# Values of all heads in one product with the tokens stationary, and an output step split behind the reciprocal

## The chip, the cores and the metric

The kernel runs on one core of a Trainium2 chip. The metric is the device time of one execution in microseconds; of several timed executions the median is given. The core's engines work side by side, each through its own queue in order: TensorE (PE, matrix products; PEld is its weight load), VectorE (DVE), ScalarE (ACT), GpSimd (POOL) and SyncE (SP, which issues the loads). A product writes to a bank of PSUM, from which VectorE or ScalarE must take the result before the bank is used again.

## The reference

The reference computes one layer of a hybrid streaming encoder for two request groups that share their weights: a prompt of 1024 tokens and a sample of 64 tokens with running state. Per layer there are three token mixers (HGRN2, a convolution, a pool mixer) from one combined input projection, then cross attention over 256 memory tokens, then an MLP with squared ReLU, each with a residual and RMS norms. What matters here is the HGRN2 mixer:

```python
z = h @ w_in
q, fl, iv, og, ca, cg, pu = jnp.split(z, IN_SPLITS, axis=-1)
...
f_gate = lbh + (1.0 - lbh) * jax.nn.sigmoid(fh)
log_f = jnp.log(jnp.maximum(f_gate, F_FLOOR))
kh = (1.0 - lbh) * jax.nn.sigmoid(-fh)
S_new, o = hgrn2_recurrence(hg_state.astype(f32), qh, kh, vh, log_f)
o = rms_norm(o, hg_norm_g.reshape(HG_HEADS, HG_DK)).reshape(B, T, HG_WIDTH)
a_out = (o * jax.nn.silu(og.astype(f32))).astype(h.dtype)
```

There are 4 heads of 128. The values `iv` are the projection's columns 1024 to 1535. The recurrence is `S_t = diag(f_t) S_{t-1} + k_t v_t^T`, `o_t = S_t^T q_t`, and each head's output is normed over its 128 channels.

## The kernel before, in words

All 1088 tokens (1024 + 64) go through one pass. Activations lie channel-major: a tile has 128 channels as partitions and the tokens as columns. Every large product is made from three products of rounded parts, high x high, high x low and low x high, so each weight tile and each activation is split into `hi` and `lo` by a ScalarE copy and a VectorE subtraction (`prep`, `hl`).

`dense` (line 210 records every product through `mm`) multiplies one block of 128 output channels: the weights are the stationary operand, the tokens stream in three groups of 364, 364 and 360 columns, and each group takes 8 blocks of input channels x 3 = 24 products into one bank `psd`. Weight tiles come by `fetch` (a load of 512 KB on SyncE's queue, four buffers `wr`) and `prep` (three buffers `wh` and `wl`); `weights` keeps up to three ready.

In `mixers` the blocks follow each other as gates of the convolution (4 dense blocks), then per head f, q and v, with the two pool inputs behind head 1, and the four output gates og. Beside these dense blocks run background chains, Python generators: `conv` (62 steps on VectorE, lines 645 and 141, tile `cacc`, then its norm), one `head` per head, and `pool` (GpSimd additions, line 137, tiles `ws` and `wu`). After each of the three column groups of a dense block `pump` advances each chain by a third of its rate: 2 for convolution and pool, 5 for a head. A newly inserted head goes to the front of the list.

A head's chain consists of these pieces, each ending in a `yield`: the diagonal scores (line 516); nine transposes of the values `vT` to token-major `vt` (lines 528, 531) with their evacuations; seven levels (line 545, with small products of lines 556 and 562), in each of which VectorE copies the scores by a mask (line 511) and multiplies `fn` and `q` by the decays `tot` before the next level can start; transposes of the keys (line 585); the chunk states `st` (line 597); and three output parts. An output part makes `o` in a bank (lines 623, 625), squares it with a sum on ScalarE, takes the root (ScalarE, which loads another table when root and sigmoid alternate), the reciprocal `hr` on VectorE (line 629), scales `o` on ScalarE, transposes it on TensorE (line 634) and evacuates it as `on`.

In the mixers no order is written out by hand. The framework's scheduler orders the instructions of each engine by its own costs and the place in the program, and the engines then run these queues strictly in order.

Of the kernel before, what the change touches and what calls it, by code (L numbers as in the profile page):

```python
# [52 lines left out]
class Trunk:  # L53
# [378 lines left out]
    def mixers(self, xs):  # L432
# [33 lines left out]
        for h in range(NH):  # L466
            sig = self.slot(n="fs")
            sgn = self.slot(n="fn")

            def evf(b, t0, m):  # L470
                self.act(sig[:, t0:t0 + m], b, AF.Sigmoid)
                self.act(sgn[:, t0:t0 + m], b, AF.Sigmoid, scale=-1.0)
            self.dense(self.weights(), xs, ks, evf)
            f = sig[:, :T]
            nc.vector.tensor_scalar(f, f, self.lb1[:, h:h + 1], self.lb[:, h:h + 1], MUL, ADD)
            nc.vector.tensor_scalar(f, f, FLOOR, None, MAX)
            nc.vector.tensor_scalar(sgn[:, :T], sgn[:, :T], self.lb1[:, h:h + 1], None, MUL)
            q = self.slot(n="q")

            def evq(b, t0, m):  # L480
                self.act(q[:, t0:t0 + m], b, AF.Sigmoid)
                self.tt(q[:, t0:t0 + m], b, q[:, t0:t0 + m], MUL)
            self.dense(self.weights(), xs, ks, evq)
            vT = self.slot(n="vT")
            self.dense(self.weights(), xs, ks, plain(vT, AF.Copy))
            self.bg.insert(0, self.chain(self.head(h, sig, sgn, q, vT, ons), 5))
            if h == 1:
                self.pool_in(xs, ks, mix)
        for h in range(NH):
# [10 lines left out]
            self.tt(mix[h][:, :T], mix[h][:, :T], ons[h][:, :T], MUL)  # L500
        return mix

    def head(self, h, f, k, q, vT, ons):
        nc = self.nc
        mm = nc.tensor.matmul
        sc = self.slot(n="sc")
# [12 lines left out]
        mm(ps[:TS, :TS], k[:, TP:T], q[:, TP:T], start=True, stop=True)  # L519
        copy_in(sc[:TS, TP:T], self.masks[:TS, 7, :TS], ps[:TS, :TS])  # L520
        yield

        vt = self.slot(n="vt")
        for j in range(2):
            ps = self.bank("m")
            for c in range(4):
                t0 = (4 * j + c) * P
                nc.tensor.transpose(ps[:, c * P:c * P + P], vT[:, t0:t0 + P], self.ident)
            self.act(vt[:, 512 * j:512 * j + 512], ps, AF.Copy)
        ps = self.bank("m")  # L530
        nc.tensor.transpose(ps[:TS, :P], vT[:, TP:T], self.ident)
        self.act(vt[:TS, TP:TP + P], ps[:TS, :P], AF.Copy)
        self.tt(q[:, :T], q[:, :T], f[:, :T], MUL)
        tot_t = self.slot(n="tot")
        tot = f[:, :T]
# [77 lines left out]
        for t0, n in SEGS:  # L613
            w = min(n, P)
            nt = n // w
            o = self.slot(n="o")
            ps = self.bank("m")
            r = self.tp.tile([P, 8], F32, tag="hr", name=self.name("hr"))
            for c in range(nt):
                s = t0 + c * P  # L620
                first = s == 0
                prev = self.state[:, h, :] if s == TP else st[:, s - P:s]
                mm(ps[:w, c * P:c * P + P], sc[:w, s:s + w], vt[:w, s:s + P], start=True, stop=first)  # L623
                if not first:
                    mm(ps[:w, c * P:c * P + P], q[:, s:s + w], prev, start=False, stop=True)  # L625
            for c in range(nt):
                self.act(o[:w, c * P:c * P + P], ps[:w, c * P:c * P + P], AF.Square, accum_out=r[:w, c:c + 1])
            self.act(r[:w, 4:4 + nt], r[:w, :nt], AF.Sqrt, scale=1.0 / P, bias=self.eps[:w])
            nc.vector.reciprocal(r[:w, 4:4 + nt], r[:w, 4:4 + nt])
            for c in range(nt):  # L630
                self.act(o[:w, c * P:c * P + P], ps[:w, c * P:c * P + P], AF.Copy, scale=r[:w, 4 + c:5 + c])
            ps = self.bank("m")
            for c in range(nt):
                nc.tensor.transpose(ps[:, c * P:c * P + w], o[:w, c * P:c * P + P], self.ident[:w, :w])  # L634
            self.act(on[:, t0:t0 + n], ps[:, :n], AF.Copy, scale=self.vec("hg_g", h))
            yield
# [575 lines left out]
    def all_weights(self):  # L1212
        a = self.a
        for o in range(8):
            yield "c", a["wk"][o]
        for k in range(8):
            yield "c", a["wv"][k]
        for o in range(22):
            yield "c", a["w_in"][o]
        for o in range(8):  # L1220
            yield "c", a["w_out"][o]
        for o in range(8):
            yield "c", a["xq"][o]
        for _ in range(2):
            for o in range(8):
                yield "c", a["xo"][o]
        for p in list(range(NPAIR)) + list(range(LATE)):
            for j in range(2):
                yield "s", a["w_up"][2 * p + j]
        for fb in FBS:  # L1230
            for o in range(4):
                yield "c", a["w_down"][fb, o]
# [36 lines left out]
def layout(i):  # L1269
    import numpy as np  # L1270

    def c(x):
        return np.ascontiguousarray(x)
# [12 lines left out]
    ca, cg, pu = [16, 17], [18, 19], [20, 21]  # L1286
    order = [cg[0], ca[0], cg[1], ca[1]]
    for h in range(NH):
        order += [f[h], q[h], v[h]]
        if h == 1:  # L1290
            order += pu
    order += og
    a["w_in"] = c(np.stack([w_in[o] for o in order]))
    a["wk"] = blocks(i["xk_w"][0])
    a["wv"] = c(i["xv_w"][0].reshape(KT, P, KT, P))
    w_out = blocks(i["w_out"][0])
# [74 lines left out]
```

## Time and profile before

| | |
|---|---|
| three timed runs, median (range) | 1576.73 us (1575.55 to 1577.51) |
| the profiled execution, its own time | 1575.83 us |
| its span in the profile | 1574.0 us |
| mean granted clock of TensorE in it | 0.991 |
| convolution steps on VectorE (line 141, `cacc`) | 60 of 1446 ns |
| VectorE busy from 160 to 200 us, 200 to 240 us | 33.9 us, 28.5 us |

A page of the profile gives busy time per engine, a chain of waits that ended last, and groups of instructions with their mean time and the idle time ahead of them. The time lines give for each instruction its start, length, engine, line, tiles written and read, and in brackets the idle time ahead of it and what ended it. Products on TensorE overlap: each lasts about twice as long as the distance between two starts. In the tables of stretches each engine has its busy time and instructions, and behind them stand the granted clock (1.00 is full speed), the share of the DMA engines and GB/s.

### The profile page before, as it was taken

To read this page: it belongs to the slowest core of one execution; us is meant where nothing else is said; L and a number is where in the kernel's file an instruction comes from. 1 tells how busy PE (TensorE), PEld (TensorE's weight loads), DVE (VectorE), ACT (ScalarE), POOL (GpSimd) and SP (SyncE) were. 2 spreads that over 40 slices of the span, in tenths; PEclk is the share of its full clock that TensorE was granted. 3 is DMA by queue.
4 is the path that set the end of the run, shared out by engine and by line. 5 is a ranking of instruction groups with operands and counts; after the bars stand their busy time and mean duration, and the time that the engine had idled before them with its cause. 6 is when DMAs were issued, how large, how long until landed. Compare 5 with 4: busy or idle time off the path is not lost.

```text
span 1574.0 us, 24480 instructions
## 1 busy us (share of the span) xinstructions
PE 1536.2 (98%) x10312; PEld 1498.8 (95%) x10312; DVE 912.9 (58%) x1305; ACT 582.8 (37%) x1054; POOL 164.1 (10%) x125
## 2 busy tenths in 40 slices
PE   7999999899999999999998999999999999999997
PEld 7799999799999999989997999999999999999997
DVE  7628879765654433584579655555585444434434
ACT  7522242445262221373455344444362121111133
POOL 0100002200000000000023422222220000000005
PEclk9999999999999999999999999999999999999998
DMA  9421000000014311222532233222386223211003
GB/s 343 144 76 42 28 31 30 29 28 31 28 52 155 132 55 54 68 68 101 181 135 96 97 111 105 104 97 87 107 303 249 104 97 111 86 65 52 31 0 115
DMA packets 54943, 150.61 MB, mean 96 GB/s; under 512 B 6704, under 2 KB 14384, under 8 KB 54832
## 3 DMA queue, kind: packets, MB, share of 16 engines
q1 hardware_dynamic: 51952, 148.37, 27.0%
q8 instruction: 81, 1.33, 0.3%
q10 hardware_dynamic: 2880, 0.66, 0.2%
q14 instruction: 30, 0.25, 0.0%
HBM read 115.11 MB, written 33.91 MB: 95 GB/s over the span
## 4 chain that ended last, share of the span: by engine, by line
PE 64%; issue 26%; DVE 6%; ACT 2%; POOL 1%; DMA 1%; SPq 0%; POOLq 0%; ACTq 0%; DVEq 0%
PE psd L210 45%; PE psm L210 12%; PE psm L545 3%; DVE cacc L141 1%; DVE wl L138 1%; POOL xr L137 1%; DVE t L141 1%; ACT hi L126 1%; DVE x L138 1%; PE psd L865 1%; PE psm L516 0%; PE psm L623 0%; DMA wr<-wk 0%; PE psm L634 0%; PE psm L625 0%
## 5 line engine op out<-in xcount | busy, mean ns | idle before, releaser
L210 PE MATMUL psd<-hi,wh 128*128 128x364 f32 (+2 forms) x1632 | 537.9, 331 | 1.5 <-ACT hi L126 0.8
L210 PE MATMUL psd<-lo,wh 128*128 128x364 f32 (+2 forms) x1632 | 538.3, 330 | 0.9 <-DVE lo L141 0.9
L210 PE MATMUL psd<-hi,wl 128*128 128x364 f32 (+2 forms) x1632 | 538.4, 330 | 0.3 <-DVE wl L138 0.3
L126 ACT ACTIVATE wh<-wr 128x1024 fp32r<-128x1024 f32 (+1 forms) x179 | 161.4, 906 | 492.8 <-PE psd L210 350.0
L210 PEld LDWEIGHTS psd<-hi,wh 128*128 128x128 f32 x1632 | 307.2, 188 | 3.6 <-ACT hi L126 1.5
L210 PEld LDWEIGHTS psd<-lo,wh 128*128 128x128 f32 x1632 | 307.8, 189 | 2.1 <-DVE lo L141 1.5
L210 PEld LDWEIGHTS psd<-hi,wl 128*128 128x128 f32 x1632 | 307.3, 188 | 1.4 <-DVE wl L138 0.6
L138 DVE TENSOR_TENSOR wl<-wr,wh 128x1024 fp32r<-128x1024 f32 (+1 forms) x179 | 189.4, 1062 | 125.5 <-ACT wh L126 125.2
L138 DVE TENSOR_TENSOR xr<-psd,xr 128x364 f32<-128x364 f32 (+3 forms) x192 | 101.9, 533 | 177.3 <-PE psd L210 177.2
L210 PE MATMUL psd<-th,wh 128*128 128x272 f32 x448 | 130.9, 292 | 3.6 <-ACT t L126 3.3
L210 PE MATMUL psd<-th,wl 128*128 128x272 f32 x448 | 130.4, 292 | 2.8 <-DVE wl L138 2.8
L210 PE MATMUL psm<-th,wh 128*128 128x272 f32 x448 | 130.4, 291 | 1.3 <-ACT t L126 0.6
L210 PE MATMUL psm<-th,wl 128*128 128x272 f32 x448 | 129.3, 290 | 0.7 <-DVE wl L138 0.7
L210 PE MATMUL psd<-tl,wh 128*128 128x272 f32 x448 | 129.5, 289 | 0.0
L210 PE MATMUL psm<-tl,wh 128*128 128x272 f32 x448 | 128.8, 288 | 0.0
L210 PEld LDWEIGHTS psd<-th,wh 128*128 128x128 f32 x448 | 84.9, 189 | 4.8 <-ACT t L126 4.3
L210 PEld LDWEIGHTS psd<-th,wl 128*128 128x128 f32 x448 | 84.8, 190 | 3.5 <-DVE wl L138 3.5
L141 DVE SCALAR_TENSOR_TENSOR cacc<-glu,vecs,cacc 128x1118 f32<-128x1118 f32 x60 | 86.8, 1446 | 0.7
L210 PEld LDWEIGHTS psm<-th,wh 128*128 128x128 f32 x448 | 84.3, 188 | 2.7 <-ACT t L126 1.4
L210 PEld LDWEIGHTS psm<-th,wl 128*128 128x128 f32 x448 | 84.1, 188 | 1.0 <-DVE wl L138 0.9
L210 PEld LDWEIGHTS psd<-tl,wh 128*128 128x128 f32 x448 | 84.9, 190 | 0.0
L210 PEld LDWEIGHTS psm<-tl,wh 128*128 128x128 f32 x448 | 84.4, 188 | 0.0
(238 smaller groups left out, 2297.6 us busy)
## 6 DMA issues: line engine op xcount, KB each, us to landing
wr<-w_up SPq DMA_DIRECT2D x38, 512.0 KB, 3.6
tt<-t SPq DMA_DIRECT2D x32, 544.0 KB, 3.1
t<-tt SPq DMA_DIRECT2D x32, 544.0 KB, 5.0
wr<-w_down SPq DMA_DIRECT2D x32, 512.0 KB, 3.3
wr<-w_in SPq DMA_DIRECT2D x22, 512.0 KB, 3.2
x<-res SPq DMA_DIRECT2D x16, 544.0 KB, 2.9
wr<-xo SPq DMA_DIRECT2D x16, 512.0 KB, 3.4
x<-xT SPq DMA_DIRECT2D x8, 544.0 KB, 8.2
```

Source lines behind the costliest of these rows:

```text
L126: return self.inorder("act", lambda: self.nc.scalar.activation(out, in_, f, **kw))
L137: return self.inorder("pool", lambda: eng.tensor_tensor(out, a, b, op))
L138: return self.inorder("dve", lambda: self.nc.vector.tensor_tensor(out, a, b, op))
L141: return self.inorder("dve", lambda: self.nc.vector.scalar_tensor_tensor(out, in0, s, in1, op0, op1))
L210: return self.inorder("pe", lambda: self.nc.tensor.matmul(*args, **kw))
L545: mm(pv[:m, c], k[:, c * P:c * P + m], qc[:, :, 1, :], start=True, stop=True)
L865: self.nc.tensor.transpose(ps[:, i * w:i * w + w], pr[:w, i, mt * P:mt * P + P], self.ident[:w, :w])
```

## The change

There are two edits, with what they entail.

The values of all heads come from one new function, `values`, that is called once, behind head 0's q. It takes four weight tiles `w_v` at once (three from the ready ones, a fourth split into two slots `wv`), and makes the product with the tokens stationary: for each of nine tiles of 128 tokens (the last of 64) and each of 8 channel blocks three products with 512 weight columns, two token tiles and two banks at a time. The result is token-major, so `vt` of each head is a copy of 128 columns from the bank; the v blocks and the transposes of `vT` go. The list of weight loads and the weight layout follow.

The head's chain gets a `yield` between the reciprocal and the scaling of `o`, so that each of the three output parts is two pieces, and its rate is 7 instead of 5.

```diff
             self.dense(self.weights(), xs, ks, evq)
-            vT = self.slot(n="vT")
-            self.dense(self.weights(), xs, ks, plain(vT, AF.Copy))
-            self.bg.insert(0, self.chain(self.head(h, sig, sgn, q, vT, ons), 5))
+            if h == 0:
+                vts = self.values(xs)
+            self.bg.insert(0, self.chain(self.head(h, sig, sgn, q, vts[h], ons), 7))
...
+    def values(self, xs):
+
+        while len(self.wq) < 3:
+            self.prep()
+        ws, self.wq = self.wq, []
+        raw = self.raws.pop(0)[1]
+        hi, lo = (self.slot(F32R, n="wv")[:, :1024].rearrange("p (k n) -> p k n", k=KT) for _ in range(2))
+        self.act(hi, raw, AF.Copy)
+        self.split_lo(lo, raw, hi)
+        self.fetch()
+        ws = [[x.rearrange("p k n -> p (k n)") for x in w] for w in ws + [(hi, lo)]]
+        vts = [self.slot(n="vt") for _ in range(NH)]
+        for c0, c1 in ((0, 2), (2, 4), (4, 6), (6, 8), (8, 9)):
+            banks = [self.bank("d") for _ in range(c0, c1)]
+            for k in range(KT):
+                wh, wl = (x[:, 512 * (k % 2):512 * (k % 2) + 512] for x in ws[k // 2])
+                for b, (t0, m) in zip(banks, TT[c0:c1]):
+                    self.mm3_t(b[:m], xs[k][0][:, t0:t0 + m], xs[k][1][:, t0:t0 + m], wh, wl, k == 0, k == KT - 1)
+            for b, (t0, m) in zip(banks, TT[c0:c1]):
+                for h in range(NH):
+                    self.act(vts[h][:m, t0:t0 + P], b[:m, h * P:h * P + P], AF.Copy)
+            self.pump(1 if c0 % 4 else 2)
+        for _ in range(2):
+            self.prep()
+        return vts
+
-    def head(self, h, f, k, q, vT, ons):
+    def head(self, h, f, k, q, vt, ons):
...
         yield
-
-        vt = self.slot(n="vt")
-        for j in range(2):
-            ps = self.bank("m")
-            for c in range(4):
-                t0 = (4 * j + c) * P
-                nc.tensor.transpose(ps[:, c * P:c * P + P], vT[:, t0:t0 + P], self.ident)
-            self.act(vt[:, 512 * j:512 * j + 512], ps, AF.Copy)
-        ps = self.bank("m")
-        nc.tensor.transpose(ps[:TS, :P], vT[:, TP:T], self.ident)
-        self.act(vt[:TS, TP:TP + P], ps[:TS, :P], AF.Copy)
         self.tt(q[:, :T], q[:, :T], f[:, :T], MUL)
...
             nc.vector.reciprocal(r[:w, 4:4 + nt], r[:w, 4:4 + nt])
+            yield
             for c in range(nt):
                 self.act(o[:w, c * P:c * P + P], ps[:w, c * P:c * P + P], AF.Copy, scale=r[:w, 4 + c:5 + c])
...
-        for o in range(22):
+        for o in range(18):
             yield "c", a["w_in"][o]
+            if o == 5:
+                for u in range(4):
+                    yield "c", a["w_v"][u]
```

The scheduler makes new queues out of this for all engines in the mixers. Three places follow. Line numbers in the changed kernel are 15 or 16 higher in the head's function (line 629 is 644, 634 is 650, 545 is 560).

VectorE, head 1, second output part. Before, from the last of the pool steps `ws` to the reciprocal of that part (the second `hr`; `fs` and `fn` are head 2's gates):

```order
L141 SCALAR_TENSOR_TENSOR ws_2167<-wu_2168,vecs,pu_1875 128x64
L141 SCALAR_TENSOR_TENSOR cacc_1829<-glu_964,vecs,cacc_1829 128x1118
L475 TENSOR_SCALAR fs_2233<-fs_2233,lbs 128x1088
L141 SCALAR_TENSOR_TENSOR cacc_1829<-glu_964,vecs,cacc_1829 128x1118
L476 TENSOR_SCALAR fs_2233<-fs_2233 128x1088
L141 SCALAR_TENSOR_TENSOR cacc_1829<-glu_964,vecs,cacc_1829 128x1118
L629 RECIPROCAL hr_2348<-hr_2348 128x4
L477 TENSOR_SCALAR fn_2234<-fn_2234,lbs 128x1088
```

The same place in the changed kernel:

```order
L138 TENSOR_TENSOR pe_2484<-wu_2317,vecs 128x16
L141 SCALAR_TENSOR_TENSOR ws_2316<-wu_2317,vecs,pu_1965 128x1008
L138 TENSOR_TENSOR ws_2316<-pe_2484,pu_1965 128x16
L141 SCALAR_TENSOR_TENSOR ws_2316<-wu_2317,vecs,pu_1965 128x64
L644 RECIPROCAL hr_2375<-hr_2375 128x4
L644 RECIPROCAL hr_2444<-hr_2444 64x1
L475 TENSOR_SCALAR fs_2397<-fs_2397,lbs 128x1088
L682 TENSOR_REDUCE lr_2526<-psm_2521 128x2
L476 TENSOR_SCALAR fs_2397<-fs_2397 128x1088
```

The convolution steps have left this place, and the reciprocals of the second and the third part now stand ahead of the steps on head 2's gates.

ScalarE, the same output part (`o`, `hr` of head 1; `fs`, `fn` the evacuations of head 2's gates). Before:

```order
L126 ACTIVATE o_2346,hr_2348<-psm_2347 128x128 x4
L126 ACTIVATE fn_2234<-psd_2384 128x360
L126 ACT_TABLE_LOAD
L126 ACTIVATE hr_2348<-hr_2348,eps 128x4
L126 ACTIVATE wh_2440<-wr_1882 128x1024
L126 ACTIVATE o_2346<-psm_2347,hr_2348 128x128 x4
```

In the changed kernel:

```order
L126 ACTIVATE o_2373,hr_2375<-psm_2374 128x128 x4
L126 ACT_TABLE_LOAD
L126 ACTIVATE fs_2397<-psd_2405 128x364
L126 ACT_TABLE_LOAD
L126 ACTIVATE hr_2375<-hr_2375,eps 128x4
L126 ACT_TABLE_LOAD
L126 ACTIVATE fn_2398<-psd_2405 128x364
L126 ACTIVATE o_2373<-psm_2374,hr_2375 128x128 x4
```

Two evacuations and three table loads now stand between the squares and the scaled copies, where one of each and a weight copy stood. On TensorE, 40 dense products lie between the last product of this part and its first transpose, and 33 lay there before.

VectorE at the end of the value product in the changed kernel (`cacc` are the convolution's two accumulators, `wl` the low parts of the next three weight tiles, `sc` and `q` head 0's):

```order
L141 SCALAR_TENSOR_TENSOR cacc_1116<-glu_788,vecs,cacc_1116 128x1118
L141 SCALAR_TENSOR_TENSOR cacc_1543<-glu_964,vecs,cacc_1543 128x1118
L138 TENSOR_TENSOR wl_1549<-wr_1159,wh_1548 128x1024
L141 SCALAR_TENSOR_TENSOR cacc_1543<-glu_964,vecs,cacc_1543 128x1118
L138 TENSOR_TENSOR wl_1555<-wr_1252,wh_1554 128x1024
L138 TENSOR_TENSOR wl_1563<-wr_1258,wh_1562 128x1024
L141 SCALAR_TENSOR_TENSOR cacc_1543<-glu_964,vecs,cacc_1543 128x1118 x2
L138 TENSOR_TENSOR tot_1613<-fs_1054 128x544
L141 SCALAR_TENSOR_TENSOR cacc_1543<-glu_964,vecs,cacc_1543 128x1118
L537 COPY_PREDICATED sc_1595<-masks,psm_1597 128x512
```

Ahead of these rows, back to the split of the third value tile (`wl_1249`), stand 31 convolution steps and the first step of the second accumulator; before, 7 such steps stood between two splits in the v block.

More of the change, by code (lines that the diff above doesn't have):

```diff
@@ L1288, in layout @@
     for h in range(NH):
-        order += [f[h], q[h], v[h]]
+        order += [f[h], q[h]]
         if h == 1:
@@ L1293, in layout @@
     a["w_in"] = c(np.stack([w_in[o] for o in order]))
+    a["w_v"] = c(i["w_in"][0][:, 1024:1536].reshape(4, 2, P, 512).transpose(0, 2, 1, 3).reshape(4, P, KT, P))
     a["wk"] = blocks(i["xk_w"][0])
```

## The prediction

> **What bounds the kernel now.** I read the page first, then the waits of TensorE in the mixer stage, then the time lines of the engines around the one large wait there. The page's first rows:
>
> ```profile
> span 1574.0 us, 24480 instructions
> PE 1536.2 (98%) x10312; PEld 1498.8 (95%) x10312; DVE 912.9 (58%) x1305; ACT 582.8 (37%) x1054; POOL 164.1 (10%) x125
> ```
>
> TensorE is busy for nearly the whole span, so a change pays only where it takes work off TensorE or ends one of its few waits. In the stretch from 80 to 470 us, which holds the edited stage, the waits of TensorE are these:
>
> ```profile
> PE psm L634 <- ACT o L126: 6.2, 2, 6.1
> ...
> PE psm L545 <- DVE q L138: 0.4, 2, 0.3
> ```
>
> One wait is the whole matter: a transpose of line 634 stands at the head of TensorE's queue until ScalarE has scaled `o`. Who was late is seen on the time lines (start, length, engine, line, tiles, idle time before):
>
> ```profile
> 279.95 0.28 ACT L126 ACTIVATE o<-psm 128x128 f32<-128x128 f32 x1
> 280.95 0.51 ACT L126 ACTIVATE fn<-psd 128x360 f32<-128x360 f32 x1
> 281.47 1.28 ACT L126 ACT_TABLE_LOAD   x1
> 282.77 0.30 ACT L126 ACTIVATE hr<-hr,eps 128x4 f32<-128x4 f32 x1
> 290.63 1.14 ACT L126 ACTIVATE o<-psm,hr 128x128 f32<-128x128 f32 x4 [6.62 <-DVE hr L629]
> ...
> 281.57 2.56 DVE L475 TENSOR_SCALAR fs<-fs,lbs 128x1088 f32<-128x1088 f32 x1
> 284.05 2.22 DVE L141 SCALAR_TENSOR_TENSOR cacc<-glu,vecs,cacc 128x1118 f32<-128x1118 f32 x1
> 286.19 3.03 DVE L476 TENSOR_SCALAR fs<-fs 128x1088 f32<-128x1088 f32 x1
> 289.14 1.37 DVE L141 SCALAR_TENSOR_TENSOR cacc<-glu,vecs,cacc 128x1118 f32<-128x1118 f32 x1
> 290.44 0.17 DVE L629 RECIPROCAL hr<-hr 128x4 f32<-128x4 f32 x1
> ...
> 280.55 3.00 POOL L137 TENSOR_TENSOR ws<-wu 128x1111 f32<-128x1111 f32 x1
> 285.15 3.49 POOL L137 TENSOR_TENSOR wu<-ws 64x1103 f32<-64x1103 f32 x1
> ...
> 291.06 0.48 PE L634 MATMUL psm<-ident,o 128*128 128x128 f32 x1 [6.07 <-ACT o L126]
> ```
>
> The root of the norm was there at 283.1, but the reciprocal of 0.17 us came at 290.4, since four long VectorE steps stood ahead of it, and three of these ran while GpSimd computed (2.56, 2.22 and 3.03 us; the fourth took 1.37). TensorE idled 6.07 us, and then its clock was down:
>
> ```profile
> 291.00:296.00 5.00, 4.95 (x16) 3.74 (x17) 3.97 (x5) 3.29 (x9) 0.00 (x0) 0.50 0.31 108
> ```
>
> The column after POOL's is the granted clock, 0.50: five microseconds at half speed lose 2.5. This one wait thus costs 6.1 + 2.5 = 8.6 us. Nothing else in the stage is worth as much, and TensorE is otherwise back to back there.
>
> **The change, term by term.** The sum is made against the profiled execution, 1575.83 us, of which 1574.0 are the span; the median of the three timed runs, 1576.73, lies 0.90 above it, and I add that at the end.
>
> *The value product, +1.2 us.* Removed are 4 heads x 3 column groups x 24 = 288 products of 364 or 360 columns; added are 9 token tiles x 8 blocks x 3 = 216 products of 512 columns. The chain of waits has both speeds (start, length, what):
>
> ```profile
> 36.55 5.47 PE psm L210 x24
> 85.89 73.38 PE psd L210 x440
> ```
>
> The first is the memory-value product, whose form (128 stationary tokens, 512 weight columns) is the new one: 0.228 us each, so 216 take 49.2. The second gives 0.1668, so 288 take 48.0. The last token tile has 64 tokens and still runs 24 full products (5.5 of the 49.2); no row shows 64 stationary columns at 512, and I take the same speed, because the columns streamed are the same. Bounds: +1 to +2.
>
> *The transposes of the values, -3.9 us.* Per head nine go (lines 528, 531):
>
> ```profile
> 165.34 1.03 PE L528 MATMUL psm<-ident,vT 128*128 128x128 f32 x8
> 166.21 0.27 PE L531 MATMUL psm<-ident,vT 128*64 128x128 f32 x1
> 166.31 1.90 PE L545 MATMUL psm<-q,fn 128*128 128x64 f32 x16
> ```
>
> From 165.34 to 166.31 are 0.97 us, four times 3.9. Their evacuations go too. The 36 new small copies out of the value product cost ScalarE about 36 x 0.28 = 10 us (row below), hidden, since ScalarE has 49 us for them and each pair of banks is read while the next pair fills.
>
> ```profile
> L126 ACT ACTIVATE o<-psm 128x128 f32<-128x128 f32 (+1 forms) x36 | 9.5, 279 | 7.8 <-PE psm L625 7.8
> L126 ACT ACT_TABLE_LOAD x18 | 23.1, 1283 | 0.3
> ```
>
> *The large wait, -8.6 us.* In the new order the reciprocal of head 1's second part stands ahead of line 475's step, with no convolution step near it: that work has moved forward into the value product, where VectorE has little else. And between the last product that feeds the squares and the first transpose stand 40 dense products (33 before): 40 x 0.1668 = 6.7 us of cover. The chain they must cover runs on ScalarE, whose order now has three table loads in it: squares 1.0 (279.95 to 280.95), 3 x 1.28, a root 0.30, two evacuations of 0.5, the first scaled copy 0.3: 6.4 us. So the wait goes, with 0.3 us to spare. If the cover failed, I would lose up to these 8.6 again (first rival).
>
> *New short waits, +3.5 us.* The chain rate of 7 instead of 5 puts a head's levels nearer to each other: mostly 14 to 17 dense products between two of them, where 20 to 24 stood. What must fit there is VectorE's predicated copy and two multiplications (the columns are the same; a copy row of x2 has a small one at its end):
>
> ```profile
> 231.43 1.38 DVE L511 COPY_PREDICATED sc<-masks,psm 128x512 f32<-128x512 uint8 x2 [1.43 <-PE psm L545]
> 232.62 0.75 DVE L138 TENSOR_TENSOR fn<-fn,fs 128x544 f32<-128x544 f32 x1
> 233.29 0.71 DVE L138 TENSOR_TENSOR q<-q,fs 128x544 f32<-128x544 f32 x1
> ...
> 238.04 1.39 DVE L138 TENSOR_TENSOR fn<-fn,tot 128x544 f32<-128x544 f32 x1
> 239.35 1.64 DVE L138 TENSOR_TENSOR q<-q,tot 128x544 f32<-128x544 f32 x1
> ...
> 244.27 0.77 DVE L511 COPY_PREDICATED sc<-masks,psm 128x512 f32<-128x512 uint8 x2
> 244.97 0.71 DVE L138 TENSOR_TENSOR fn<-fn,tot 128x544 f32<-128x544 f32 x1
> 245.60 0.71 DVE L138 TENSOR_TENSOR q<-q,tot 128x544 f32<-128x544 f32 x1
> ...
> 236.47 2.38 POOL L137 TENSOR_TENSOR ws<-pu 128x1117 f32<-128x1117 f32 x1 [22.38 <-ACT pu L126]
> ```
>
> In the first two levels this takes 231.43 to 234.0 = 2.6 us, in the others 244.27 to 246.3 = 2.0. The cover is a small product of 0.2 and 15 x 0.167 = 2.5, together 2.7. So the later levels are covered, and the first two of each head are short by perhaps 0.15 with the hand-over: 8 x 0.15 = 1.2. While GpSimd runs, two multiplications take 3.0 instead of 1.4 (1.39 and 1.64): GpSimd's pooling now meets head 1's levels with 14 products between them, one or two of which I charge 0.8 in all. The other output steps have covers near their chains (head 1's last part 28 products, 4.7 us, against two table loads and the rest, about 5): 1.2. At the end of the value product 31 convolution steps stand on VectorE ahead of the split of the next weights:
>
> ```profile
> 146.65 9.89 DVE L141 SCALAR_TENSOR_TENSOR cacc<-glu,vecs,cacc 128x1118 f32<-128x1118 f32 x7
> 246.24 1.37 DVE L141 SCALAR_TENSOR_TENSOR cacc<-glu,vecs,cacc 128x1118 f32<-128x1118 f32 x1
> 247.53 1.21 DVE L138 TENSOR_TENSOR wl<-wr,wh 128x1024 fp32r<-128x1024 f32 x1
> ```
>
> At 1.40 each (9.89 / 7, one accumulator) they take 43 of the 49 us, and the split would come about 1 us late; at 1.29 each (246.24 to 247.53, a step that doesn't use the one before; the two accumulators now alternate) it is in time. I take 0.3, near the second. Sum 1.2 + 0.8 + 1.2 + 0.3 = 3.5; bounds 0 and 10 (0.35 at each of 28 level steps).
>
> *The clock after short waits, +0.5 us.* Before the mixers two waits close together brought the clock down:
>
> ```profile
> 57.00:60.00 3.00, 1.42 (x5) 0.64 (x5) 3.00 (x3) 0.90 (x1) 0.00 (x0) 1.00 0.03 11
> 60.00:64.00 4.00, 4.00 (x12) 2.65 (x10) 2.73 (x3) 2.15 (x2) 0.00 (x0) 0.58 0.36 131
> ```
>
> 1.58 us idle of 3, and then a clock of 0.58 over 4 us, a loss of 1.7. I charge 0.5: such a bunch is likely once in three. Bounds 0 and 3.4. The Trainium skill's page "TensorE: Matmul & The Clock Gate" (section "Why this matters for your kernels") wants idle gaps kept under about 3 us, and by that gaps of a few tenths would cost nothing of the clock: the sum would be 0.5 lower. The trace's 1.58 us disagree with the bare threshold, so I keep the 0.5.
>
> *At nothing:* ScalarE's six table loads more (6 x 1.28 us; ScalarE is busy 37% of the span, and where they lie in a chain they are counted above); the loads, as many and as large as before and in the same queue; the stages behind the mixers, whose order on each engine is unchanged but for a few places at their start, where the splits of the last mixer rows come earlier than they are used.
>
> Sum: 1.2 - 3.9 - 8.6 + 3.5 + 0.5 = -7.3. From 1575.83 that is 1568.5, and 1569.4 on the scale of the median; I say **1569.5 us**, 0.46% faster.
>
> **The rivals.**
>
> *No new waits* (20%): the order that sets the distances has priced the level steps well, as before the change, where all of them together made TensorE wait 0.4 us (row L545 above). Then 1576.73 + 1.2 - 3.9 - 8.6 = 1565.4. Against it: the distances are shorter by a third.
>
> *The value product ends in a wait* (13%): VectorE at 1.40 us a step reaches the next weights 1.2 us late, and as the split of the following weights and head 0's first steps queue behind it, the same is paid twice more, and one drop of the clock is sure (1.7 in place of the 0.5): 3 x 1.2 - 0.3 + 1.2 = 4.5 on top: 1574.
>
> *The large wait only moves* (12%): the ScalarE chain of 6.4 us meets anything slow, such as VectorE steps stretched to 2.56 and 3.03 us by GpSimd, and the transpose waits as long as before. The -8.6 is gone: 1578, no change that can be told.
>
> *The levels starve TensorE, slower* (10%): this decides once VectorE's step between two levels exceeds 2.7 us throughout and not in the first two levels alone, because convolution, GpSimd and splits get into each. Short by 0.7 at 28 level steps is 20 us, and two clock drops 3.4: 1576.73 - 11.3 + 20 + 3.4 is 1589. At 0.4 it is 1580. For it speaks the 93% of VectorE in 130 to 160 us (27.78 of 30); against it, that the convolution is done earlier now, so that heads 1 to 3 have VectorE nearly to themselves.
>
> ```profile
> 130.00:160.00 30.00, 30.00 (x185) 30.00 (x185) 27.78 (x25) 7.22 (x13) 0.00 (x0) 1.00 0.15 51
> ```
>
> **How the numbers follow.** The forecast has 45%. A measurement of this kernel tells about 0.2%, 3.2 us, from no change. Faster by more: the forecast, "no new waits" and half of the value-product case: 0.71. Within: the other half and most of the moved wait: 0.17. Slower: the starved levels and what is left of the moved wait: 0.12. The range reaches from 1564.5, just below the case without new waits, to 1577.5, where the moved wait begins; beyond lie the starved levels and part of the moved wait, some 2 in 10. The forecast's own range is 1566 to 1573.
>
> **What would show it.** Right: no wait of line 650 (the old 634) over 1 us and no clock of 0.5 in the f and q products of head 2; 24 value products in about 5.5 us; no transposes of vT; the mixer stage some 7 us shorter, and all later stages as long as before. Wrong: level products (line 560) waiting for VectorE by more than 3 us in all, a wait of the dense products for `wl` or `wh` right behind the value product, or a clock at half outside the old place.

## The result, and the profile after

Five timed runs of the changed kernel have a median of 1567.94 us (1566.51 to 1568.42), five of the kernel before 1576.73 us (1575.55 to 1577.51). The ratio is 0.9946 (95% interval 0.9935 to 0.9958): 8.8 us, 0.54% faster. The forecast was 1569.5 us.

The head of the page of the kernel after:

```profile
span 1564.7 us, 24291 instructions
PE 1530.6 (98%) x10204; PEld 1484.5 (95%) x10204; DVE 905.9 (58%) x1305; ACT 587.5 (38%) x1072; POOL 162.6 (10%) x125
```

There are 108 products fewer (288 + 36 gone, 216 come). The waits of TensorE between 80 and 470 us, in the kernel after (who waited, for whom: us in all, times, the longest):

```profile
PE psm L560 <- DVE q L138: 2.3, 1, 2.3
PE psd L210 <- DVE lo L141: 0.9, 2, 0.5
PE psd L210 <- ACT hi L126: 0.8, 1, 0.8
```

The wait of 6.1 us is gone, a new one of 2.3 us is there, at a level of head 1, and the other two rows stood there before. The new wait on the time lines of the kernel after (start, length, engine, line, tiles):

```profile
262.92 2.07 POOL L137 TENSOR_TENSOR ws<-pu 128x1117 f32<-128x1117 f32 x1 [13.78 <-ACT pu L126]
263.00 3.07 DVE L138 TENSOR_TENSOR wl<-wr,wh 128x1024 fp32r<-128x1024 f32 x1
...
265.99 0.77 DVE L537 COPY_PREDICATED sc<-masks,psm 128x512 f32<-128x512 uint8 x2
...
267.10 2.42 POOL L137 TENSOR_TENSOR wu<-ws 64x1115 f32<-64x1115 f32 x1
267.54 2.56 DVE L138 TENSOR_TENSOR q<-q,tot 128x544 f32<-128x544 f32 x1
...
270.25 1.97 PE L560 MATMUL psm<-q,fn 128*128 128x64 f32 x16 [2.30 <-DVE q L138]
```

A multiplication of 0.71 us took 2.56, and it ended 0.58 us after the GpSimd sum that had begun before it. The clock took no harm from this wait. During the old one a stretch at half clock had begun, from 289.35 to 296.18 us, with TensorE busy in 5.1 of its 6.8 us. Stretches of the kernel before, around the end of the old wait, and of the kernel after, behind the new one (the columns are those of the prediction's windows, the granted clock the third number from the end):

```profile
289.30:296.10 6.80, 5.04 (x17) 3.84 (x18) 5.77 (x7) 3.75 (x10) 0.00 (x0) 0.50 0.23 80
```

```profile
270.00:275.00 5.00, 4.75 (x35) 4.67 (x35) 2.15 (x5) 0.00 (x0) 0.00 (x0) 1.00 0.00 0
```

To set kernels against each other I take the length of the mixers from the first evacuation into `csig` to the first into `res`. Before, and after:

```profile
86.59 0.84 ACT L126 ACTIVATE csig<-psd 128x364 f32<-128x364 f32 x2 [2.14 <-PE psd L210]
...
469.20 0.54 DVE L138 TENSOR_TENSOR res<-psd,res 128x364 f32<-128x364 f32 x1 [1.53 <-PE psd L210]
```

```profile
88.04 0.84 ACT L126 ACTIVATE csig<-psd 128x364 f32<-128x364 f32 x2 [2.14 <-PE psd L210]
...
460.38 0.54 DVE L138 TENSOR_TENSOR res<-psd,res 128x364 f32<-128x364 f32 x1 [3.00 <-PE psd L210]
```

That is 382.61 and 372.34 us: the mixers are 10.3 us shorter. The two profiled executions (1575.83 and 1566.53) are 9.3 us apart: the changed kernel begins its mixers 1.45 us later, behind one stretch of half clock more (at 44.4 us), and behind them it is 0.5 us shorter, with one such stretch fewer (at 559.0 us in the kernel before). The last section shows that these come and go with no edit at all. In the mixers the measure repeats: the changed kernel gave 372.4 again in a second profile, two profiles of the variant without the split gave 371.9 and 372.0, and two of the variant with VectorE's pooling gave 369.9 and 370.0. So the mixers' length tells tenths of a microsecond apart where the total tells two microseconds.

### The profile page after: what moved, and what is told of

It is laid out like the page before. It is cut to its first block, busy times and chain, and to the rows that moved or that the text cites. A ratio compares the mean times of both kernels' runs of the same rounds, so it can differ in the third digit from the quotient of the medians.

```text
span 1564.7 us, 24291 instructions
## 1 busy us (share of the span) xinstructions
PE 1530.6 (98%) x10204; PEld 1484.5 (95%) x10204; DVE 905.9 (58%) x1305; ACT 587.5 (38%) x1072; POOL 162.6 (10%) x125
## 3 DMA queue, kind: packets, MB, share of 16 engines
q8 instruction: 80, 1.31, 0.3%
## 4 chain that ended last, share of the span: by engine, by line
PE 66%; issue 26%; DVE 4%; ACT 2%; POOL 1%; DMA 1%; SPq 0%; POOLq 0%; ACTq 0%; DVEq 0%
PE psd L210 46%; PE psm L210 13%; PE psm L560 3%; DVE wl L138 1%; POOL xr L137 1%; ACT hi L126 1%; PE psm L638 1%; DVE t L141 1%; DVE x L138 1%; PE psm L612 0%; PE psm L640 0%; PE psd L881 0%; PE psm L542 0%; DMA wr<-wk 0%; ACT L126 0%
## 5 line engine op out<-in xcount | busy, mean ns | idle before, releaser
L210 PE MATMUL psd<-lo,wh 128*128 128x364 f32 (+3 forms) x1536 | 505.9, 329 | 0.9 <-DVE lo L141 0.9
L210 PE MATMUL psd<-hi,wl 128*128 128x364 f32 (+3 forms) x1536 | 506.4, 330 | 0.3 <-DVE wl L138 0.3
L210 PE MATMUL psd<-hi,wh 128*128 128x364 f32 (+3 forms) x1536 | 504.9, 330 | 1.5 <-ACT hi L126 0.8
L210 PEld LDWEIGHTS psd<-hi,wh 128*128 128x128 f32 x1536 | 288.4, 188 | 3.5 <-ACT hi L126 1.5
L210 PEld LDWEIGHTS psd<-lo,wh 128*128 128x128 f32 x1536 | 288.7, 188 | 2.2 <-DVE lo L141 1.5
L210 PEld LDWEIGHTS psd<-hi,wl 128*128 128x128 f32 x1536 | 288.6, 188 | 1.4 <-DVE wl L138 0.6
L141 DVE SCALAR_TENSOR_TENSOR cacc<-glu,vecs,cacc 128x1118 f32<-128x1118 f32 x60 | 80.6, 1378 | 0.5
```

The lines of the kernel that those rows point to most:

```text
L141: return self.inorder("dve", lambda: self.nc.vector.scalar_tensor_tensor(out, in0, s, in1, op0, op1))
L210: return self.inorder("pe", lambda: self.nc.tensor.matmul(*args, **kw))
```

## The experiments

My theory was that the gain is one wait: VectorE's queue stood ahead of a reciprocal, and GpSimd made that queue slow. The rivals were that the value product itself is the gain, or the split of the output step.

| kernel | ratio to before (95%) | mixers, us | of it lost to half clock, us | waits in the mixers, us |
|---|---|---|---|---|
| before | 1 | 382.6 | 2.6 | 6.1 at L634 |
| split alone | 0.9996 (0.9988 to 1.0004) | 381.9 | 2.2 | 5.4 at the transposes, 1.1 at levels |
| rate 7 alone | 1.0011 (1.0002 to 1.0019) | 382.6 | 1.5 | 4.1 at L745, 1.2 at L634, 0.8 at levels |
| split, rate 7 | 1.0033 (1.0020 to 1.0045) | 387.5 | 6.4 | 3.7 at the transposes, 2.3 at a level, 0.6 at a bank |
| value product alone | 1.0026 (1.0013 to 1.0038) | 389.2 | 10.8 | 2.8 and 1.4 at levels, 1.4, 0.9 and 0.6 at banks, 0.3 at the transposes |
| value product, rate 7 | 0.9933 (0.9920 to 0.9947) | 371.9 | 0 | 0.6 and 0.3 |
| all three (the change) | 0.9946 (0.9935 to 0.9958) | 372.3 | 0 | 2.3 at a level |

The fourth column is half of TensorE's busy time in the stretches at half clock within the mixers, since what it idles there is counted among the waits. Single waits under 0.3 us are mostly left out; the 0.9 and 0.8 us at line 210 lie ahead of the first evacuation into `csig` in each kernel. The eighth combination, the value product with the split and the rate of 5, was not run, and the mixers of the kernel before and of the four variants that are no faster come from one profile each.

**GpSimd's sums taken from the kernel before.** The sums and copies are cut to their first 64 columns and the two long reads of them go to `pu`; the kernel leaves the rest of the pooling out, so its output is not the layer's. The edit, likewise in every sum and copy:

```diff
+        z = 64
...
-        self.tt(s[:, 1:n], pu[:, 1:n], pu[:, 0:n - 1], ADD, gp)
+        self.tt(s[:, 1:z], pu[:, 1:z], pu[:, 0:z - 1], ADD, gp)
...
-        self.stt(d[:, 16:TP], res[:, PH + 16:PH + TP], self.vec("inv_w", c), pu[:, PH + 16:PH + TP], MUL, SUB)
+        self.stt(d[:, 16:TP], pu[:, PH + 16:PH + TP], self.vec("inv_w", c), pu[:, PH + 16:PH + TP], MUL, SUB)
```

> The kernel before, with GpSimd's pooling sums cut to the first 64 of 1118 columns (the rest of the pooling is left out; the order of TensorE's products is the same row for row). The theory of the wait: the reciprocal of head 1's second part comes late because four VectorE steps stand ahead of it and GpSimd stretches three of them. Alone these steps take 0.84 + 1.37 + 0.71 + 1.37 = 4.3 us in place of 9.2, so the wait at line 634 falls from 6.1 to about 1.6 us and the half clock behind it (2.5 us) goes: 1576.7 - 4.5 - 2.5 = 1569.7, or 1572.2 if the clock still falls. The theory of the order alone: the steps stand ahead of the reciprocal whatever GpSimd does, the wait stays at 5 to 6 us and the time at 1576. The theory that the gain of the change is one of the value product, not of the wait: 1576.7 as before.

Measured: a ratio of 0.9921 (0.9907 to 0.9935), median 1562.21 beside 1574.30. The same four VectorE steps on the time lines of this kernel, with the reciprocal behind them:

```profile
277.81 0.84 DVE L475 TENSOR_SCALAR fs<-fs,lbs 128x1088 f32<-128x1088 f32 x1
...
278.57 1.40 DVE L141 SCALAR_TENSOR_TENSOR cacc<-glu,vecs,cacc 128x1118 f32<-128x1118 f32 x1
...
279.89 0.74 DVE L476 TENSOR_SCALAR fs<-fs 128x1088 f32<-128x1088 f32 x1
...
280.56 1.41 DVE L141 SCALAR_TENSOR_TENSOR cacc<-glu,vecs,cacc 128x1118 f32<-128x1118 f32 x1
...
281.89 0.17 DVE L629 RECIPROCAL hr<-hr 128x4 f32<-128x4 f32 x1
...
283.27 0.27 PE L634 MATMUL psm<-ident,o 128*128 128x128 f32 x1
```

From the first of them to the reciprocal are 4.1 us, where 8.9 stood before (281.57 to 290.44), and line 634 does not wait at all. The order of TensorE's products is that of the kernel before, the reciprocal stands behind the same four steps, and the mixers take 372.8 us: 9.8 us less, nearly the change's 10.3, with no change of TensorE's order. So in this order GpSimd's running sums are the cause of the large wait, and the order alone is not. The two gains are not of one kind: here all but half a microsecond is waits and half clock, while in the change 3.5 us are less work for TensorE. One size was off: I expected 1.6 us to stay and 7 us to be gained in all. The mixers gained 9.8, with the half clock gone whole and the short waits at line 545 too. What I had overlooked is a fifth step that GpSimd held up, ahead of the four, in the kernel before:

```profile
278.42 2.05 POOL L137 TENSOR_TENSOR wu<-ws 128x1115 f32<-128x1115 f32 x1 [8.60 <-DVE ws L138]
278.48 3.16 DVE L141 SCALAR_TENSOR_TENSOR cacc<-glu,vecs,cacc 128x1118 f32<-128x1118 f32 x1
```

Without the sums this step takes 1.38 us, and line 475's step starts 0.2 us before the first square and not 1.6 behind it (277.81 against 277.99, and 281.57 against 279.95). These 1.8 us and the 4.8 between the first step and the reciprocal are more than the whole wait of 6.1. The median gained 12.1; the profiled execution, 1568.49, was the slowest of the five (the others 1561.6 to 1563.5), so what the other four saved outside the mixers stays open.

**The same in the kernel after.** The edit is the same.

> The kernel after with GpSimd's pooling sums cut to the first 64 of 1118 columns (the rest of the pooling is left out). What is tested is the wait of 2.3 us left at a level of head 1 (line 560), ahead of which VectorE's multiplication took 2.56 us beside a GpSimd sum and the split of the weights 3.07. By the theory of GpSimd's stretching it goes, and the time is 2.3 lower, 1565.6. By the theory that the levels stand too close it stays at 2 us or more: 1567.9.

Measured: 0.9926 (0.9913 to 0.9939) to the kernel before; mixers 370.0 us, 2.3 less than the kernel after. Its waits from 80 us to 475:

```profile
PE psd L210 <- DVE lo L141: 0.9, 2, 0.5
PE psd L210 <- ACT hi L126: 0.8, 1, 0.8
```

The 2.3 us are gone, to the tenth. The levels, mostly 14 to 17 products apart, make TensorE wait for nothing else.

**The split and the rate, without the value product.** Lines of the kernel before:

```diff
             nc.vector.reciprocal(r[:w, 4:4 + nt], r[:w, 4:4 + nt])
+            yield
...
-            self.bg.insert(0, self.chain(self.head(h, sig, sgn, q, vT, ons), 5))
+            self.bg.insert(0, self.chain(self.head(h, sig, sgn, q, vT, ons), 7))
```

The first edit alone:

> The kernel before with the split of the output step alone, rate 5 and values by head. In this order line 475's step, line 476's, line 477's and a convolution step stand ahead of head 1's second reciprocal. If the split alone covers the wait: a ratio of 0.994 to 0.996 (1568 to 1570 on the scale of 1576.7). If the wait is VectorE's queue beside GpSimd, the split only gives it more products to hide behind while the reciprocal comes later still: the wait stays at 2 to 5 us, 0.998 to 1.001.

The second alone:

> The kernel before with the chain rate of 7 alone, values by head, no split. With it the cube of the three parts is nearly whole. If the rate needs the value product (which moves the convolution ahead of the heads): the convolution still stands among head 0's and head 1's levels, these lie 14 to 16 products apart, GpSimd's sums meet them, and the kernel is no faster: a ratio to before of 0.999 to 1.004. If the rate alone removes the large wait, since in this order the next head's gate steps stand behind head 1's reciprocals: 0.994 to 0.997.

Both:

> The kernel before with two parts of the change alone: the output step split behind the reciprocal, and the chain rate 7; values by head and transposes of vT as before. The theory of the wait: in this order the reciprocal of head 1's second part stands ahead of line 475's step and 43 dense products cover the rest, so the wait of 6.1 us and the half clock go (-8.6); the convolution now shares the levels' shorter distances (14 to 16 products, 2.5 us, against 2.0 of level work and a convolution step of 1.37), which costs 0 to 0.9 at each of some 14 levels, say 4: 1572 (1568 to 1577). The theory of the value product: the order gains nothing, 1577 to 1580.

None of the three is faster. The split alone leaves a wait of 5.4 us at the same transposes, as its text had it. The rate alone moves the wait to line 745, the pooling's product. Both together are slower, which I had not expected: I had 1568 to 1577 us and in this scale it is 1582. The waits of that kernel, and its time lines ahead of the larger one:

```profile
PE psm L635 <- ACT o L126: 3.7, 1, 3.7
PE psm L545 <- DVE tot L138: 2.3, 1, 2.3
```

```profile
282.04 3.06 POOL L137 TENSOR_TENSOR wu<-ws 128x1115 f32<-128x1115 f32 x1 [1.58 <-DVE st L141]
...
283.11 2.01 DVE L138 TENSOR_TENSOR pe<-wu,vecs 128x16 f32<-128x16 f32 x1
...
285.17 3.03 POOL L137 TENSOR_TENSOR ws<-wu 128x1111 f32<-128x1111 f32 x1
...
286.23 2.01 DVE L138 TENSOR_TENSOR ws<-pe,pu 128x16 f32<-128x16 f32 x1
```

Two VectorE steps of 16 columns took 2.01 us each (0.14 and 0.17 in the kernel after, where no sum ran), and each ended 0.02 to 0.04 us after the GpSimd sum beside it. They stand ahead of the reciprocal in this order. I had counted the convolution among the levels and not what GpSimd would meet.

**The value product alone, and with the rate.** Lines of the kernel after:

```diff
-            self.bg.insert(0, self.chain(self.head(h, sig, sgn, q, vts[h], ons), 7))
+            self.bg.insert(0, self.chain(self.head(h, sig, sgn, q, vts[h], ons), 5))
...
             nc.vector.reciprocal(r[:w, 4:4 + nt], r[:w, 4:4 + nt])
-            yield
```

Without the rate and the split:

> The kernel after with the chain rate back at 5 and without the split of the output step: the value product alone. If the product itself removes the large wait (its pumps move the convolution ahead of the heads, so that VectorE's queue is short when head 1's reciprocals come): -2.7 for product and transposes, -6.1 for the wait and -1.7 to -3.4 for the clock, short waits as before: a ratio to the kernel before near 0.993 (1565 on the scale of 1576.7), as with the rate of 7. If the rate of 7 is needed to keep the heads apart from the next head's gate steps: the wait returns with 3 to 6 us, 0.997 to 0.998 (1573).

Without the split alone:

> The kernel after without the split of the output step: the value product and the chain rate 7 alone. The theory of the wait: the product and the transposes give -2.7, and in this order no long VectorE step stands ahead of head 1's reciprocals, so the large wait is gone too (-8.6); but only 13 to 17 products (2.2 to 2.8 us) cover squares, root, reciprocal and scaled copies (some 2 us, and a table load of 1.28 or two), so most output steps wait 0.5 to 1.5 us: 8 of them, some 5 in all, 1570 (1567 to 1574), and the split is worth 2 us. The theory of the value product: 1568, as with the split, since the split hides nothing. A theory of the split (the large wait went because of it): the wait is back with 4 to 6 us and the time near 1574.

The first came out slower than before, 1.0026, and neither of its two expectations holds. The large wait is gone as the first of them says, but others come late in the stage. Its waits, and the windows where they lie (TensorE's and VectorE's busy time are the first and the third number behind the length):

```profile
PE psm L560 <- DVE q L138: 2.8, 2, 2.0
...
PE psm L577 <- DVE sc L537: 1.4, 1, 1.4
PE psd L210 <- DVE og L138: 1.4, 1, 1.4
```

```profile
405.00:412.00 7.00, 5.01 (x34) 4.08 (x32) 2.13 (x6) 4.42 (x13) 0.00 (x0) 1.00 0.03 11
412.00:420.00 8.00, 5.23 (x22) 4.35 (x22) 4.00 (x9) 1.28 (x4) 0.00 (x0) 0.53 0.00 0
420.00:433.00 13.00, 12.95 (x47) 12.25 (x48) 4.56 (x8) 3.69 (x7) 0.00 (x0) 0.50 0.00 1
```

With the 12 column groups of the v blocks and their pumps gone and the rate still 5, the heads fall behind: two levels of head 3 (at 407.8 and 413.4 us) follow each other with no dense product between them, TensorE waits for VectorE inside the first and ahead of the second, and from 412.4 us on the clock stays at half for 20.5 us, 18.1 of them with TensorE busy. GpSimd does nothing there. So the rate of 7 by itself is not what gains; it gives back to the heads the steps that the vanished blocks took from them. With it and without the split the kernel is as fast as the change, or faster: 0.9933.

**Is the split worth anything?** The change itself and the same without the split, on one chip:

> The changed kernel itself, on the chip of the three kernels beside it, so that they can be set against it directly: 0.9946 of the kernel before, as measured.

> The changed kernel without the split of the output step, beside the changed kernel. If the split hides a wait of the output steps: 1 to 2 us slower than the kernel after. If it hides nothing and only sets where the pooling's sums fall among the levels: 1 to 2 us faster (the wait of 2.3 us did not stand in the trace without the split); within 0.1% it can't be told.

Measured: 0.9943 (0.9931 to 0.9955) and 0.9940 (0.9927 to 0.9953), medians of 1566.03 and 1565.70. The totals can't tell them apart. In the mixers the variant without the split is 0.4 us shorter (372.0 against 372.4): it has no wait of 2.3 us, and these waits in its place (80 to 475 us):

```profile
PE psm L760 <- DVE ws L141: 0.7, 1, 0.7
PE psm L649 <- ACT o L126: 0.3, 1, 0.3
```

So 10 to 31 dense products were enough for the output steps but for the 0.3 us. Both had the same sums on GpSimd, only at other moments, and the wait of 2.3 us that stands with the split alone covers what else the split may be worth; the next experiments, where the sums are off GpSimd, show this better.

**The pooling's sums on VectorE.** The sums are the same, on another engine; nothing is left out. The edit in the kernel after:

```diff
-        gp = nc.gpsimd
+        gp = nc.vector
...
-            gp.tensor_copy(u[:64, 3:n], s[:64, 3:n])
+            self.act(u[:64, 3:n], s[:64, 3:n], AF.Copy)
...
-            gp.tensor_copy(u[:64, PH:n], s[:64, PH:n])
+            self.act(u[:64, PH:n], s[:64, PH:n], AF.Copy)
```

> The kernel after with the pooling's sums on VectorE and its two copies on ScalarE in place of GpSimd: the same result, and GpSimd idle in the mixers but for clearing sc. VectorE's sums take about 0.7 to 1.3 us each, six of them; the order puts them behind head 1's levels and between its output steps. By the theory of GpSimd's stretching the 2.3 us wait goes: 2 to 3 us faster than the kernel after, a ratio to before of 0.993 (1565.5). By the theory that VectorE is then too full: a wait of 1 to 2 us at head 1's output steps in its place, 0.995.

And without the split:

> The kernel after without the split of the output step and with the pooling's sums on VectorE, the copies on ScalarE. The split was worth nothing that showed (ratio 0.9933 without it, 0.9946 with it on another chip), and without it no wait of 2.3 us stood in the trace; so the sums on VectorE have only the waits of 0.6 and 0.3 us at lines 760 and 649 to gain or to lose: a ratio to before of 0.992 to 0.994. If six more VectorE steps among head 1's reciprocals, with only 13 to 17 products to cover each output step, make these late: 0.995 to 0.996.

Both gave 0.9929 (0.9915 to 0.9943, and 0.9914 to 0.9945). In the mixers they differ: 370.9 us without the split, with a wait of 0.5 us at line 649, and 369.9 with it. So with GpSimd's sums out of the way the split is worth 1.0 us there (one profile without it, two with it), too little for the totals to show. The first was then set beside the change on one chip:

> The changed kernel with the pooling's sums on VectorE and the two copies on ScalarE, beside the changed kernel. By the traces the wait of 2.3 us is gone and nothing has come in its place: 2.3 us faster, a ratio of 0.9985 to the kernel after and 0.993 to the kernel before. If the difference between the two was one between chips: equal.

Measured: 0.9935 (0.9923 to 0.9948), median 1564.15 beside 1566.03 of the change. The mixers are 2.4 us shorter, in both profiles of it, and its list of waits there is that of the kernel after without GpSimd's sums. So the wait is gone as expected and nothing came in its place in this stage: a sum on VectorE takes 1.31 us and lies where no product waits. In the total the advantage over the change is 1.9 us with intervals that overlap, so that it beats the change is likely and not shown. Against the kernel before it is the same gain as the change's, or a little more.

## Why the prediction was right

**The value product, +1.2 us: right.** In the kernel after, line 210's products alone, in 45 us of the value product:

```profile
145.00:190.00 45.00, 45.00 (x200) 36.71 (x199) 1.00 0.03 12
```

From one start to the next are 0.2272 us on the mean, 216 take 49.1, against 48.0 for the 288 before: +1.1. The 24 products of the last token tile, with 64 tokens, start 0.230 us apart, hardly more. ScalarE's small copies stayed hidden.

**The transposes, -3.9 us: right.** By start-to-start times the 36 took 3.84 us.

**The large wait, -8.6 us: right.** It is gone, 6.1 us, and with it the stretch at half clock, in which TensorE was busy for 5.1 us: 2.6 lost, against 2.5 in the sum. The working was that the long VectorE steps leave the reciprocal and the cover of 40 products (6.7 us) then meets a ScalarE chain of 6.4. The time lines of the kernel after show that chain:

```profile
296.21 0.28 ACT L126 ACTIVATE o<-psm 128x128 f32<-128x128 f32 x1 [0.65 <-PE psm L640]
...
300.78 0.18 DVE L644 RECIPROCAL hr<-hr 128x4 f32<-128x4 f32 x1 [6.45 <-ACT hr L126]
...
302.43 1.13 ACT L126 ACTIVATE o<-psm,hr 128x128 f32<-128x128 f32 x4
...
302.84 0.33 PE L650 MATMUL psm<-ident,o 128*128 128x128 f32 x1
```

From the first square to the end of the first scaled copy are 6.5 us, the reciprocal follows its root at once, VectorE having been idle for 6.45, and the first transpose starts with no wait that the list shows. The cause behind it was told as GpSimd stretching VectorE; the experiment on the kernel before shows that the wait goes with the sums alone, and that a fifth step belonged to it. Why VectorE is free at that moment was right too. The convolution's steps, in the view of the tile `cacc`, before and after (ns: least, median, longest; then when the first and the last began):

```profile
L141 DVE SCALAR_TENSOR_TENSOR cacc<-glu,vecs,cacc x60: 1354/1376/3164, 122.4 to 302.8; 128x1118 f32<-128x1118 f32 x60
```

```profile
L141 DVE SCALAR_TENSOR_TENSOR cacc<-glu,vecs,cacc x60: 1354/1378/1387, 123.8 to 247.5; 128x1118 f32<-128x1118 f32 x60
```

They now end at 249 us, ahead of GpSimd's first sum at 262.9, and none of them is longer than 1.39 us. It is the value product that moves them: with it alone the last begins at 257.0 us and the large wait is gone, with the rate alone at 301.5. What the prediction did not say is that the gain takes the product and the rate together: neither alone makes the kernel faster.

**New short waits, +3.5 us: too large, and wrong in its parts.** This is the step that failed. I spread it over 8 level steps (1.2), other output steps (1.2), the end of the value product (0.3) and GpSimd at head 1's levels (0.8). Measured are 2.3 for the last and nothing that the list shows for the others. The levels' covers were long enough, and the term for GpSimd was three times too small. I had priced it as a slowing (two multiplications at 3.0 for 1.4 us), where the rows already told of a stop: in the prediction's own time lines the steps of 2.56 and 3.03 us end at 284.13 and 289.22, each 0.58 after the GpSimd sum beside it (283.55 and 288.64), and so does the multiplication of 1.39 us that I priced by (239.43, the sum 238.85). A convolution step, 1.37 us alone, ends 1.17 us after the sum that it met (281.64, the sum 280.47), and the steps of 16 columns 0.02 to 0.04: each ends a little less than its own length behind the sum, as a step does that starts when the sum is over. So the price of a meeting is what is left of the sum, up to 2.5 us, and not a factor on the step. The Trainium skill's page "SBUF — State Buffer" (section "Who interferes with whom") has that rule: VectorE and GpSimd share a pair of ports that one of them holds for a whole instruction, while the other is fully blocked, if VectorE's instruction has two inputs in SBUF or works in a mode with two ports. The trace agrees, four times with 0.58 us; weighed in the prediction, the rule would have priced the level at a whole sum.

**The clock after short waits, +0.5 us: it cost nothing** in the mixers of the kernel after. The wait of 2.30 us left the clock whole, while in the kernel with the split and the rate one of 2.34 us was followed by 6.8 us at half, and in the kernel with the value product alone two of 1.4 and 2.0 us came with 20.5 us at half. The rule of the Trainium skill that the prediction names (page "TensorE: Matmul & The Clock Gate", section "Why this matters for your kernels": no idle gaps over about 3 us) holds for the first and not for the others. Seen in the steps of 3.413 us of the last section, the 2.34 us lie within one step and the 2.30 in two, 1.75 and 0.55; but 1.58 us of idle time in one step were followed by half clock ahead of the mixers of the kernel before, so idle time in a step doesn't decide by itself. What decides there stays open.

The sum in the mixers, from TensorE's busy time (the first number behind the length) before and after:

```profile
86.59:469.20 382.61, 375.88 (x2497) 360.80 (x2496) 259.95 (x372) 141.67 (x329) 21.68 (x13) 0.99 0.10 34
```

```profile
88.04:460.38 372.34, 369.82 (x2386) 346.09 (x2385) 251.67 (x372) 146.75 (x347) 19.48 (x13) 1.00 0.11 35
```

TensorE idles 6.7 and 2.5 us (-4.2), loses 2.6 and nothing to half clock (-2.6), and the rest is its work, 373.3 and 369.8 (-3.5): together the -10.3 that is measured, where the forecast had -7.3. Of the 3.5, products and transposes explain 2.7 (+1.1 - 3.8); no run shows where the other 0.8 comes from. The later stages were to be as long as before, and in the two profiled executions they are within 0.5 us (with stretches at half clock that cost 5.6 us before and 3.9 after there, by TensorE's busy time). That the total, 8.8 us, came nearer to the forecast than the mixers did is at least in part luck: in the profiled execution the mixers began 1.45 us later, for the one stretch of half clock ahead of them.

**The rivals.** "No new waits" was nearest: the levels' distances had been set well, but for GpSimd. The value product does not end in a wait: the two rows at line 210, 0.9 and 0.8 us, are those of the kernel before. The large wait did not move in the change; among its parts it stayed at the transposes with the split alone (5.4 us) and with split and rate (3.7), and moved to line 745 with the rate alone (4.1). Starved levels came in one kernel, that with the value product and the old rate, and with small waits, 2.8 + 1.4 us; what makes that kernel slower are the 10.8 us lost to half clock in the mixers, against 2.6.

## What to carry to other kernels

Ahead of a change of order, look for long steps of one engine that end at the same distance after another engine's: that is a block, and shortening the blocker may bring as much as a reordering (9.8 us beside 10.3 here, by leaving the sums out; moving them to VectorE was tried in the kernel after alone). A change of several parts is one change when they feed the same background work: here the product with the old rate loses time, the rate with the old products gains none, and only the pair gains. Where the total moves by a microsecond or two for no reason that the kernel has, compare the length of the edited stage between two fixed instructions.

## What the runs showed that was not expected

TensorE's clock can fall with no wait at all. The end of the residual stage in the kernel with VectorE's pooling: the 3.4 us ahead, the 3.4 us at half clock, and the products of one column that stand there, from 545 to 553 us:

```profile
545.25:548.66 3.41, 3.41 (x26) 3.31 (x26) 1.57 (x4) 0.41 (x2) 0.00 (x0) 1.00 0.40 141
```

```profile
548.70:552.10 3.40, 3.40 (x17) 3.40 (x16) 0.00 (x0) 0.60 (x1) 0.00 (x0) 0.50 0.03 5
```

```profile
L210 PE MATMUL psm<-ones,acc 128*128 128x1 f32 (+1 forms) x18 | 2.2, 246 | 0.0
```

TensorE is busy throughout, in the stretch ahead too, and the same products ran at full clock in the kernel after. All stretches at half clock, in every profile, are 3.41 us or a multiple of it long (but for the last, which the end of the kernel may cut), and within a profile they begin whole multiples of 3.413 us from one another: in the kernel before at 60.7, 289.3, 559.0, 716.0 and 859.4 us, which are 0, 67, 146, 192 and 234 such steps. The Trainium skill's page "TensorE: Matmul & The Clock Gate" (section "What's actually happening") says that the clock is judged in windows of 3413 ns that run freely and don't start with the kernel; the trace agrees. It makes plain why two profiles of the same kernel differ: the variant with VectorE's pooling took 1562.16 us with one such stretch between the mixers and the last stage, and 1565.36 with four, while TensorE had been busy much alike ahead of the second of them (3.81 and 3.84 us of the five from 700 us). For the residual stage the 14 profiles bear out that the place of the window decides: the 18 products of one column take 2.15 us, and where 2.04 us or more of them fall into one step, the next step is at half clock (nine profiles), and where the border parts them, with at most 1.95 us in one step, it is not (five). For the other places this is argued, and no run moved a step on purpose.
